# A 4096 x 4096 x 4096 matmul with bias and tanh: the first bias load, the matmuls on zeros, the place of one sum, and the order of all engines

## The chip, the cores and the metric

The kernel runs on one NeuronCore of a Trainium2 chip, in one launch. The metric is the device time of one execution in microseconds (us), as the median of several runs. The core has a matrix engine (TensorE, PE in the profile, with its weight loads as PEld), a vector engine (VectorE, DVE), a scalar engine (ScalarE, ACT), GpSimd (POOL) and SyncE (SP). Here GpSimd issues all loads of `a` and `b` from the inputs (converting them to fp16 on the way), and SyncE issues all other transfers: the bias, stores of results, and intermediate tiles to and from DRAM. Both feed the core's 16 DMA engines.

## The reference

```python
m, k, n = 4096, 4096, 4096
a = np.random.randn(m, k).astype(np.float32)
b = np.random.randn(k, n).astype(np.float32)
bias = np.random.randn(n).astype(np.float32)

def reference(a, b, bias):
    return np.tanh(np.matmul(a, b) + bias)
```

## The kernel before

**Arithmetic.** The kernel multiplies in fp16 with fp32 sums, by a scheme of the Strassen-Winograd kind: a 2 x 2 block product with seven products P1 to P7 in place of eight. The left operands are a11, a12, a22 and the sums s1 to s4 (s1 = a21 + a22, s2 = s1 - a11, s3 = a11 - a21, s4 = a12 - s2); the right ones are b11, b21, b22 and the sums t1 to t4. P1 = a11 b11, P2 = a12 b21, P3 = s4 b22, P4 = a22 t4, P5 = s1 t1, P6 = s2 t2, P7 = s3 t3. A product is either *plain* (for two row pairs, 2 x 16 matmuls of 128 x 128 by 512 columns, L832) or *fine*: the scheme is used once more inside it, with 7 x 8 matmuls of 256 columns (L847), and VectorE and ScalarE then make the inner sums (`fine_left`, `fine_right`).

**Tiling.** The columns of the output are cut into four chunks of 1024. The rows are cut into 16 pairs, and two pairs make a *duo*, eight in all.

- *Opening* (to about 121 us): the first eight row blocks of chunk 0 are computed by ordinary matmuls (L2049), while loads are short. It begins with `WARM` matmuls on a tile of zeros (L1968). Then come the first four tiles of each of four row blocks: they are loaded as `first` (L1975), turned on TensorE (L2088), copied out of PSUM by ScalarE and VectorE (L2094), and multiplied. Further rows are loaded as `land` and turned on VectorE (L506).
- *Chunk 0* (to about 404 us): the six remaining duos, in the order `ORDER[0]`. `STEEP[0]` says how many of a duo's products are fine: 1 means P1; 2 means P1 and P7; 3 means P1, P7 and P5. For each duo the rows of `a` are loaded (`nat`, L530), turned on VectorE and summed. s2 is made in the place of a11, and a copy of it goes to DRAM for the later chunks (`keep`, `move`, L594). s4 is made in `work`, when P3's turn comes, and is written over s2.
- *Chunks 1 and 2* (to about 1078 us) are done together, with 512-column matmuls inside fine products (L1572). They go product by product over all duos in `WIDE_ORDER`.
- *Chunk 3*: `pass_one` (P1, P2 and P6 of all duos) and `pass_two` (P7, P5, P4 and P3), in `ORDER[3]` and its reverse. Partial results wait in a tile `st` per duo; the last `HOLD` duos of the first pass keep it on the chip, the others send it to DRAM. In the second pass a duo has a `p7` and a `cs` tile besides. With `TOGETHER[3]` = n the last n duos of the second pass are run product by product, not duo by duo.

**What sets the order.** The code does not emit instructions directly. It adds operations to a `Plan`: engine, guessed duration, what is read and written, bytes. The plan gives each a due time, counted back from the end, and then plays the whole kernel through with its guesses: on each engine it takes the ready operation that is due first and for which there is room. Room is `PLACES` = 51 places of 4 KB per partition. From this come the order of the instructions on every engine and the place of each buffer. So a changed constant can move instructions everywhere. `WARM_TIME`, `RATES`, `SLACK` and the rest are guesses that enter only this play. `WIDE_EARLY`, `FARTHER` and the like say how far ahead of TensorE a load may be taken up. The chip knows only the resulting order on each engine and the waits that follow from what the operations read and write. An `after=` in `add` counts in the play alone, and makes no wait on the chip.

**Where the change sits.** `load_bias` (L919) is called for chunk 0 with `after=plan.last_pe`, when the first products of the opening have been added. `take_up` and `after_p1` are its first users. `KEEP_AT` says after which duo of chunk 0 the operands of the first two pairs go to DRAM: those pairs were turned in the opening (tiles named `o`).

Of the kernel before, what the change touches and what calls it, by code (L numbers as in the profile page):

```python
# [10 lines left out]
P = 128  # L11
QP = 32
NB = 512
NH = NB // 2
NCW = 2 * NB
# [1 line left out]
TB = 4  # L17
TP = T // 2
G = 2
WARM = 24  # L20
fp32 = mybir.dt.float32
fp16 = mybir.dt.float16
pair32 = mybir.dt.uint32
# [1 line left out]
SUB = mybir.AluOpType.subtract  # L25
# [5 lines left out]
KEPT = (('a11', 'a12'), ('s1', 'a22', 's4'), ('a11', 'a12', 's3', 's2', 's1', 'a22', 's4'), ())  # L31
NEAR = 10.0
REACH = 15.0
ORDER = ((2, 3, 4, 5, 6, 7), (7, 0, 4, 2, 6, 1, 3, 5), (2, 1, 4, 0, 3, 5, 6, 7), (7, 6, 5, 4, 0, 2, 1, 3))
LASTING = ((), (), (), ())
SHARED = True
SOFT = 1.5
BEHIND = 2
FARTHER = (50, 65, 40, 50)
THREE = (False, True, True, True)  # L40
AFTER = (6, 6, 6, 7)
HOLD = (1, 1, 1, 3)
KEEP_AT = (0, 1)
NAT_LEAD = 2.0
FIRST = (0, 1)
WHOLE = ()
# [2 lines left out]
HELD = ("s1", "s3", "s4")  # L49
PLAIN = (0, 0, 0, 0)  # L50
SMALL = 4
OVER = True
TWICE = True
RING = 8
SPEED, SLACK = 1.0, 0.8
# [8 lines left out]
    ((0.32, 0.40, 0.45), (0.47, 0.55, 0.54)),  # L64
)
FIRST_AT = 1.4
WARM_TIME = 7.6
RISE = ((), (4, 4, 4, 4, 4, 4, 4, 4), (4, 4, 4, 4, 4, 4, 4, 4), (4, 4, 4, 4, 4, 4, 4, 4))
SECONDS = (0, 8, 8, 8)
STEEP = ((0, 1, 2, 2, 2, 3), (), ())  # L70
BASIS = ("a11", "a12", "a22", "s2")
STORED = BASIS + ("s1", "s3", "s4")
LEFT = ('P6', 'P7', 'P5', 'P4', 'P3')
Q_ORDER = (0, 2, 1, 3)
WIDE = 1
WIDE_LASTING = ('s3', 's1')
TOGETHER = (0, 0, 0, 0)
WIDE_ORDER = (7, 6, 1, 5, 4, 3, 2, 0)
WIDE_PASSES = ((("P1", 0),), (("P2", 0),), (("P6", 0), ("P7", 1)), (("P4", 0),), (("P5", 0), ("P3", 1)))
TURN = 5  # L80
WIDE_EARLY = {'P1': (11.0, 80), 'P2': (11.0, 90), 'P6': (11.0, 100), 'P7': (8.0, 120), 'P4': (11.0, 70), 'P5': (11.0, 50), 'P3': (18.0, 100)}


class Buf:
# [74 lines left out]
class Plan:  # L159
# [14 lines left out]
    def add(self, eng, dur, emit, reads=(), writes=(), nbytes=0, hw=True, soft=None, early=0.0, lead=0.0, reach=1e9, after=None, long=False):  # L174
        early, far = early if isinstance(early, tuple) else (early, self.FAR)
        op = Op()
        op.n, op.eng, op.dur, op.emit = len(self.ops), eng, dur, emit
        op.nbytes, op.hw, op.soft, op.early, op.lead = nbytes, hw, soft, early, lead
        op.parts = 4 if dur > 1 and not hw else 1
        op.reach, op.far = reach, far  # L180
        if nbytes:
            kind = ("POOL", "LONG")[long] if not hw else "out" if soft is not None else "in"
            rate, wait = RATES[self.open][kind]
            op.flow, op.wait = nbytes / (rate * SPEED), wait + SLACK
            op.share = SHARES[self.open][long]
            op.kind = 0 if soft is None else 2 if writes else 1
        op.lag = op.wait + op.flow if nbytes else self.LATE
        preds, seen = set(), {}
        for group, writing in ((reads, False), (writes, True)):
            for access in group:  # L190
                buf, atoms = access if isinstance(access, tuple) else (access, access.atoms)
                if isinstance(buf, Bank):
                    if eng == "PE":
                        preds |= buf.rest
                        buf.rest = set()
                        buf.pe = op
                        buf.writer, buf.readers = {}, {}
                        continue
                    if buf.pe:
                        preds.add(buf.pe)  # L200
                    buf.rest.add(op)
                else:
                    seen[buf] = True
                for i in atoms:
                    if i in buf.writer:
                        preds.add(buf.writer[i])
                    if writing:
                        preds.update(buf.readers.get(i, ()))
                        buf.writer[i], buf.readers[i] = op, []
                    else:  # L210
                        buf.readers.setdefault(i, []).append(op)
        if after:
            preds.add(after)
        preds.discard(op)
        op.bufs = [b for b in seen if b.cls]
        for b in op.bufs:
            b.users += 1
        if eng == "PE":
            if self.last_pe:
                preds.add(self.last_pe)  # L220
            self.last_pe = op
        op.preds = preds
        op.succs = []
        for p in sorted(preds, key=lambda p: p.n):
            p.succs.append(op)
        self.ops.append(op)
        return op
# [181 lines left out]
def kernel(  # L409
# [7 lines left out]
    nc = tc.nc  # L417
# [43 lines left out]
    LO, HI = ds(0, NH), ds(NH, NH)  # L461
# [4 lines left out]
    def dve(n, emit, reads, writes, wide=False, **kw):  # L466
        add("DVE", 0.08 + n / (960 if wide else 1900), emit, reads, writes, **kw)
# [14 lines left out]
    ALL = slice(None)  # L482
# [137 lines left out]
    def asum(s, name, x, y, op, over=None, **kw):  # L620
        x, y = s[x], s[y]
        s[name] = s[over] if over else new(name, [P, T, P], atoms=2)
        tt(at(s[name]), at(x), at(y), op, T * P, (x, y), (s[name],), wide=False, **kw)
# [289 lines left out]
    def load_bias(c, after=None):  # L913
        k = {}
        k["b1"] = new("bias", [P, 2, NB], fp32, atoms=2)
        src = bias[ds(c * NCW, NCW)]
        add(
            "SP", 0.34,
            lambda: nc.sync.dma_start(  # L919
                out=k["b1"][ALL].rearrange("P a b -> P (a b)"),  # L920
                in_=bass.AP(tensor=src.tensor, offset=src.offset, ap=[[0, P], *src.ap]),
            ),
            (), (k["b1"],), nbytes=P * NCW * 4, after=after,
        )
        return k

# [19 lines left out]
    def work(duo, name, s, part=None, last=True):  # L946

        d, c, k, bop, pair = duo, duo.c, duo.k, duo.bop, duo.pairs[s]
        left, right, bank = {
            "P1": ("a11", "b11", D), "P2": ("a12", "b21", D), "P7": ("s3", "t3", I), "P6": ("s2", "t2", Z),  # L950
            "P5": ("s1", "t1", C), "P3": ("s4", "b22", C), "P4": ("a22", "t4", Z),
        }[name]
        bank = bank[s]
        a_ = d.a[s]
        if name == "P3" and "s4" not in a_:
            asum(a_, "s4", "a12", "s2", SUB, over=None if d.stays else "s2")
            if "s4" in d.put:
                put_by(d, "s4", s)
                if s:
                    sigma("s4", pair // 2, d.a, 12.0)  # L960
        t0, nt = (0, T) if part is None or name == "P3" else (part * TP, TP)
        start = name == "P1" or (name == "P7" and part != 1)
        product(bank, a_[left], [bop.get((right, i)) for i in range(4)], t0, nt, start)
        b1 = k["b1"]
        if name == "P1":
            after_p1(d, s, part)
        elif name == "P7":
            if part != 0:
                d.p7[s] = new("p7", [P, NB], fp32, "out")
                copy(at(d.p7[s]), at(bank), NB, (bank,), (d.p7[s],))  # L970
                after_p7(d, s, part)
        elif name == "P6":
            after_p6(d, s, part)
        elif name == "P5":
            if part == 0:
                return
            after_p5(d, s)
        elif name == "P2":
            if part == 0:
                e = d.aside[s] = [new("aside", [P, NB], fp32, "out" if i == 2 else "big") for i in range(0)]  # L980
                d.as11[s] = (d.box[s], 0)
                copy(at(d.box[s], ALL, 0), at(bank), NB, (bank,), ((d.box[s], (0,)),))
            else:
                finish(bank, 2 * pair, c * NCW)
        elif name == "P3":
            finish(bank, 2 * pair, c * NCW + NB)
        elif name == "P4":
            if part == 0:
                box, low = d.box[s], d.low
                tt(at(low, ALL, s), at(bank), at(box, ALL, 0), SUB, NB, (bank, (box, (0,))), ((low, (s,)),))  # L990
                tt(at(box, ALL, 1), at(C[s]), at(box, ALL, 0), SUB, NB, (C[s], (box, (0,))), ((box, (1,)),))
            else:
                finish(bank, 2 * pair + 1, c * NCW)
# [280 lines left out]
    def third(c, pq, pairs, fine):  # L1274

        duo = min(pairs) // 2
        after = c + 1 < NC and RISE[c + 1][ORDER[c + 1][::-1].index(duo)] < 4
        if {"P7", "P4"} <= set(fine) and {("a22", duo), ("s2", duo)} <= skewed and not after:
# [686 lines left out]
    def warm():  # L1965
        ps = psum.tile([P, NB], fp32, name="warm", tag="ps_0")
        for i in range(WARM):
            nc.tensor.matmul(ps[ALL], zeros[ALL, :P], zeros[ALL], start=i == 0, stop=i == WARM - 1)  # L1968

# [176 lines left out]
    for p in FIRST:  # L2146
# [3 lines left out]
        firsts[p] = s  # L2150
        if not KEEP_AT[p]:
            keep(p, s)
# [8 lines left out]
    k, before, held = k0, None, None  # L2161
    for c in range(NC):
# [14 lines left out]
        if c >= TWO:  # L2177
            plan.open = 2
            k = load_bias(c)
# [27 lines left out]
        for i, pairs in enumerate(duos):  # L2207
            d = Duo()
# [6 lines left out]
            over = OVER and 0 < i < len(duos) - 1  # L2215
# [68 lines left out]
```

## Time and profile before

| | |
|---|---|
| time before, median of 3 runs | 1433.62 us (1432.93 to 1434.62) |
| the profiled execution: its own time | 1433.78 us |
| the profiled execution: span, first to last instruction | 1432.1 us |
| TensorE matmuls | 1422.2 us busy, 99% of the span |
| VectorE | 1078.1 us, 75% |
| ScalarE | 392.8 us, 27% |
| GpSimd | 325.3 us, 23% |
| DMA | 399.19 MB, mean 279 GB/s |

The times in rows of the profile are microseconds from the start of the span. A timeline row gives the start, the length, the engine, the source line, the operation, `out<-in` by tile names without numbers, and how many instructions the row stands for. In brackets is how long the engine was idle before it, and what ended that. A wait on several things is put down to the one that came last. `SPq` rows are the issues of transfers by SyncE's queue. Lines of one helper (L473 is VectorE's two-operand operation, L476 ScalarE's copy) serve many purposes, so the tile names tell them apart. The ends of matmuls are modelled; their starts are not.

### The profile page before, as it was taken

What the parts mean: (1) busy time and instruction counts of PE and PEld (TensorE: products, weight loads), DVE (VectorE), ACT (ScalarE), POOL (GpSimd) and SP (SyncE); (2) the same over time, 40 slices, a digit from 0 to 9 for tenths busy, and PEclk for the clock granted to TensorE, in tenths of its full rate; (3) what the DMA queues carried; (4) which work ended last, traced back from release to release, by engine and by line L of the source; (5) the groups of instructions that cost most, each with busy time, mean ns of one, the idle gap of its engine ahead of it and who ended that gap; (6) DMA issues with size and microseconds to landing.
All of it is one profiled execution on the core that took longest, in us unless ns stands there. A gap on an engine that the chain in (4) does not pass through costs nothing.

```text
span 1432.1 us, 22563 instructions
## 1 busy us (share of the span) xinstructions
PE 1422.2 (99%) x8408; PEld 822.2 (57%) x8408; DVE 1078.1 (75%) x1594; ACT 392.8 (27%) x746; POOL 325.3 (23%) x613
## 2 busy tenths in 40 slices
PE   9999999999999999999999999999999999999998
PEld 4444555555644444444444444444447888888887
DVE  3359968767985376796568787988798689997876
ACT  3111212221333333311111133233233332244433
POOL 8764332334452341100111130000130300000000
PEclk9999999999999999999999999999999999999999
DMA  9999998899999899997899799899999987788883
GB/s 188 178 236 286 251 293 196 222 240 221 274 276 316 235 274 302 280 358 290 265 291 294 270 294 389 341 367 344 334 335 354 271 248 265 250 297 286 304 301 134
DMA packets 167486, 399.19 MB, mean 279 GB/s; under 512 B 25425, under 2 KB 44369, under 8 KB 167377
## 3 DMA queue, kind: packets, MB, share of 16 engines
q1 hardware_dynamic: 104400, 318.03, 61.2%
q0 software_dynamic: 62976, 79.73, 33.4%
q8 instruction: 66, 1.08, 0.3%
q14 instruction: 44, 0.35, 0.1%
HBM read 327.68 MB, written 149.68 MB: 333 GB/s over the span
## 4 chain that ended last, share of the span: by engine, by line
PE 76%; DMA 2%; DVE 1%; POOL 0%; issue 0%; ACT 0%; SPq 0%; DVEq 0%
PE ps L1572 45%; PE ps L847 25%; PE ps L832 6%; DMA nat<-in_a_dram 1%; DMA xa<-a 1%; DMA s<-a 1%; DVE a L473 0%; POOL nat L530 0%; DVE s L473 0%; DVE a L506 0%; DVE u L473 0%; ACT parts L1370 0%; DVE ys L473 0%; DVE parts L473 0%; DVE za L684 0%
## 5 line engine op out<-in xcount | busy, mean ns | idle before, releaser
L759 POOL DMA_DIRECT2D b<-in_b_dram x320 | 169.7, 535 | 607.7 <-DMA out_dram<-u 163.6
L476 ACT COPY ps<-ps 128x256 f32<-128x256 f32 (+1 forms) x216 | 100.8, 467 | 443.0 <-PE ps L1572 306.0
L530 POOL DMA_DIRECT2D nat<-in_a_dram x224 | 118.5, 533 | 208.8 <-DMA nat<-in_a_dram 51.6
L473 DVE TENSOR_TENSOR u<-ps,u 128x512 f32<-128x512 f32 x160 | 106.1, 686 | 26.2 <-PE ps L1572 25.1
L473 DVE TENSOR_TENSOR parts<-ps,parts 128x512 f32<-128x512 f32 (+1 forms) x129 | 72.6, 563 | 67.2 <-PE ps L1572 40.0
L832 PEld LDWEIGHTS <-a 128*128 128x128 f16 x704 | 68.8, 98 | 81.9 <-issue 2.4
L473 DVE TENSOR_TENSOR ps<-ps,parts 128x256 f32<-128x256 f32 (+1 forms) x151 | 82.7, 552 | 39.4 <-PE ps L1572 22.0
L2049 PE MATMUL ps<-b,o 128*128 128x512 f16 x512 | 111.3, 379 | 0.1
L476 ACT COPY parts<-ps 128x256 f32<-128x256 f32 (+1 forms) x151 | 69.0, 461 | 135.9 <-DVE ps L473 45.6
L1572 PE MATMUL ps<-b,zs 128*128 128x512 f16 x448 | 105.8, 379 | 0.0
L1572 PEld LDWEIGHTS <-ya 128*128 128x128 f16 x624 | 61.1, 98 | 73.6
L506 DVE STREAM_TRANSPOSE a<-nat 128x512 uint32<-128x512 uint32 x112 | 73.2, 690 | 20.8 <-DMA nat<-in_a_dram 17.4
L832 PE MATMUL ps<-b,a 128*128 128x512 f16 x384 | 84.7, 379 | 2.1 <-DVE parts L473 2.1
L1572 PEld LDWEIGHTS <-zs 128*128 128x128 f16 x512 | 50.1, 98 | 60.2
L1572 PEld LDWEIGHTS <-xa 128*128 128x128 f16 x512 | 50.1, 98 | 60.2
L2049 PEld LDWEIGHTS <-o 128*128 128x128 f16 x512 | 49.8, 98 | 60.3 <-ACT o L2094 0.5
L494 ACT ACTIVATE parts<-ps 128x512 f32<-128x512 f32 x52 | 31.0, 597 | 162.4 <-PE ps L832 98.1
L1572 PE MATMUL ps<-b,za 128*128 128x512 f16 x320 | 75.6, 379 | 0.0
L473 DVE TENSOR_TENSOR b<-b,b 128x2048 f16<-128x2048 f16 (+2 forms) x76 | 68.0, 910 | 10.1 <-DMA b<-in_b_dram 9.5
L832 PE MATMUL ps<-t,a 128*128 128x512 f16 x320 | 72.3, 379 | 0.0
L1572 PEld LDWEIGHTS <-za 128*128 128x128 f16 x384 | 37.6, 98 | 45.3
L847 PEld LDWEIGHTS <-ya 128*128 128x128 f16 x592 | 57.9, 98 | 7.1
(163 smaller groups left out, 2560.1 us busy)
## 6 DMA issues: line engine op xcount, KB each, us to landing
b<-in_b_dram POOLq DMA_DIRECT2D x320, 128.0 KB, 8.0
ya<-a SPq DMA_DIRECT2D x70, 512.0 KB, 7.2
xa<-a SPq DMA_DIRECT2D x70, 512.0 KB, 7.2
u<-U SPq DMA_DIRECT2D x62, 512.0 KB, 6.6
nat<-in_a_dram POOLq DMA_DIRECT2D x224, 128.0 KB, 8.0
U<-u SPq DMA_DIRECT2D x48, 512.0 KB, 6.9
ys<-s SPq DMA_DIRECT2D x46, 512.0 KB, 5.0
xs<-s SPq DMA_DIRECT2D x46, 512.0 KB, 5.6
```

The costliest lines, as they stand in the source:

```text
L473: dve(n, lambda: nc.vector.tensor_tensor(out=o(), in0=x(), in1=y(), op=op), reads, writes, wide, **kw)
L476: act(n, lambda: nc.scalar.copy(o(), x()), reads, writes, **kw)
L494: act(NB, lambda: nc.scalar.activation(o[ALL], src[ALL], TANH), (src,), (o,), soft=2.0)
L506: nc.vector.transpose(dst[ALL].rearrange("P t m -> P (t m)").bitcast(pair32).rearrange("P (U m) -> P U m", m=P)[:, ds(t0 // 2, nu), ds(row ...
L530: nc.gpsimd.dma_start(out=tl[(ds(q * QP, QP), *key)], in_=src)
L759: nc.gpsimd.dma_start(out=dst.rearrange("p t j n -> p t (j n)") if j is None else dst, in_=src)
L832: nc.tensor.matmul(bank[ALL], left_tile(left, k + t + shift), rb.tile(t), start=start and k == t0 and t == 0, stop=k + t == t0 + nt - 1, s ...
L847: nc.tensor.matmul(bank[ALL, HALF[half]], left_tile(buf, at_ * TP + i * TB + t), rb.tile(t), start=False, stop=i == 1 and t == TB - 1, ski ...
L1572: nc.tensor.matmul(bank[ALL, cols], left_tile(buf, at_ * TP + i * TB + t), rb.tile(t, half), start=start and not (i or t), stop=i == 1 and ...
L2049: nc.tensor.matmul(bank[ALL], left_tile(left, t), rb.tile(tb), start=start, stop=stop, skip_group_check=True,)
```

## The change

- The first chunk's bias: a memset of 256 columns of the bias tile is added on VectorE, planned after the last TensorE operation added so far, and the load writes the same tile, so that the load waits for the memset. The load itself no longer carries `after`.
- `WARM` goes from 24 to 18 matmuls on zeros, and its guessed time from 7.6 to 6.3 us.
- s4 in chunk 0 is written over a12, not over s2.
- `STEEP[0]`: the third duo has one fine product in place of two.
- `KEEP_AT`: the operands of pair 1 go to DRAM when they are made, not after the first duo.
- `ORDER[3]`, `TOGETHER[3]`, `FARTHER[3]`, three entries of `WIDE_EARLY`, and no `SLACK` on transfers in the opening: they act through the plan alone.

```diff
-WARM = 24
+WARM = 18
...
-ORDER = ((2, 3, 4, 5, 6, 7), (7, 0, 4, 2, 6, 1, 3, 5), (2, 1, 4, 0, 3, 5, 6, 7), (7, 6, 5, 4, 0, 2, 1, 3))
+ORDER = ((2, 3, 4, 5, 6, 7), (7, 0, 4, 2, 6, 1, 3, 5), (2, 1, 4, 0, 3, 5, 6, 7), (5, 2, 1, 4, 0, 6, 7, 3))
...
-FARTHER = (50, 65, 40, 50)
+FARTHER = (50, 65, 40, 40)
...
-KEEP_AT = (0, 1)
+KEEP_AT = (0, 0)
...
+S4_OVER = 'a12'
...
-WARM_TIME = 7.6
+WARM_TIME = 6.3
...
-STEEP = ((0, 1, 2, 2, 2, 3), (), ())
+STEEP = ((0, 1, 1, 2, 2, 3), (), ())
...
-TOGETHER = (0, 0, 0, 0)
+TOGETHER = (0, 0, 0, 3)
...
-WIDE_EARLY = {'P1': (11.0, 80), 'P2': (11.0, 90), ..., 'P3': (18.0, 100)}
+WIDE_EARLY = {'P1': (14.0, 100), 'P2': (11.0, 50), ..., 'P3': (14.0, 90)}
...
-            op.flow, op.wait = nbytes / (rate * SPEED), wait + SLACK
+            op.flow, op.wait = nbytes / (rate * SPEED), wait + SLACK * (self.open > 0)
...
         k["b1"] = new("bias", [P, 2, NB], fp32, atoms=2)
         src = bias[ds(c * NCW, NCW)]
+        if after:
+            dve(NH, lambda: nc.vector.memset(k["b1"][ALL, 0, HI], 0.0), (), (k["b1"],), after=after)
         add(
             "SP", 0.34,
...
-            (), (k["b1"],), nbytes=P * NCW * 4, after=after,
+            (), (k["b1"],), nbytes=P * NCW * 4,
...
         if name == "P3" and "s4" not in a_:
-            asum(a_, "s4", "a12", "s2", SUB, over=None if d.stays else "s2")
+            asum(a_, "s4", "a12", "s2", SUB, over=None if d.stays else S4_OVER)
```

More of the change, by code (lines that the diff above doesn't have):

```diff
@@ L80 @@
 TURN = 5
-WIDE_EARLY = {'P1': (11.0, 80), 'P2': (11.0, 90), 'P6': (11.0, 100), 'P7': (8.0, 120), 'P4': (11.0, 70), 'P5': (11.0, 50), 'P3': (18.0, 100)}
+WIDE_EARLY = {'P1': (14.0, 100), 'P2': (11.0, 50), 'P6': (11.0, 100), 'P7': (8.0, 120), 'P4': (11.0, 70), 'P5': (11.0, 50), 'P3': (14.0, 90)}
 class Buf:
```

## The prediction

> **What bounds the kernel now.** I read the page first, then the list of what TensorE (PE) waited for, and then the timeline around each of those waits.
>
> ```profile
> span 1432.1 us, 22563 instructions
> PE 1422.2 (99%) x8408; PEld 822.2 (57%) x8408; DVE 1078.1 (75%) x1594; ACT 392.8 (27%) x746; POOL 325.3 (23%) x613
> ...
> PE ps L832 <- DVE parts L473: 2.1, 1, 2.1
> PE ps L847 <- DVE a L473: 1.7, 1, 1.7
> PE warm L1968 <- DVE zeros L1962: 1.4, 1, 1.4
> PE ps L847 <- ACT ps L476: 0.4, 1, 0.4
> ```
>
> TensorE is busy for 1422.2 of 1432.1 us, so the kernel is bound by its matmuls and only 9.9 us are idle. The list names 5.6 of them: 1.4 before the first matmul on zeros, two stalls in the first chunk (2.1 and 1.7) and one of 0.4 near the start of the last chunk. Most of the rest is the tail behind the last matmul, which this change does not shorten. So whatever the new order does, it can win only three things: fewer or cheaper matmuls, the head, and 4.2 us of stalls. It can lose anything, since an order set anew can bring new stalls in any stage.
>
> The profiled execution took 1433.78 us, 1.68 more than its span. I make the sum against 1433.78 and take off 0.16 at the end, the distance to the median of 1433.62. About 0.2% (2.87 us) is what a measurement of this kernel can tell from no change, so faster means below 1430.75 and slower above 1436.49.
>
> **The matmuls: a step of STEEP.** The third duo of chunk 0 goes from two fine products to one, so its P7 becomes plain. The timeline shows both kinds back to back:
>
> ```profile
> 317.54 10.52 PE L832 MATMUL ps<-b,a 128*128 128x512 f16 x48
> 327.90 1.04 PE L847 MATMUL ps<-b,a 128*128 128x256 f16 x8
> 328.78 1.04 PE L847 MATMUL ps<-f1t,ys 128*128 128x256 f16 x8
> ```
>
> By starts, 48 plain matmuls take 327.90 - 317.54 = 10.36 us, 0.2158 each; 8 fine ones 0.88 us, about 0.1093 each over longer runs. The fine P7 is 7 x 8 = 56 matmuls, 6.12 us; the plain one 2 x 16 = 32, 6.91 us. That is **+0.79 us**, all on TensorE and so on the path. No other constant changes the number of products. In exchange VectorE (DVE) loses the duo's fine left sides; the splitting of t3 for the first fine P7 is not saved, it moves to the next duo.
>
> **The two stalls in chunk 0: s4 in a12's place.** The timelines around them:
>
> ```profile
> 239.04 1.96 SPq L594 DMA_DIRECT2D s<-a  x1
> 250.45 1.23 DVE L473 TENSOR_TENSOR a<-a,a 128x2048 f16<-128x2048 f16 x1 [4.55 <-DMA s<-a]
> 251.59 0.68 DVE L473 TENSOR_TENSOR parts<-ps,parts 128x512 f32<-128x512 f32 x1
> 252.33 3.61 PE L832 MATMUL ps<-b,a 128*128 128x512 f16 x16 [2.11 <-DVE parts L473]
> 254.78 3.67 POOL L530 DMA_DIRECT2D nat<-in_a_dram  x7 [9.62 <-DVE parts L473]
> ...
> 272.53 1.30 DVE L506 STREAM_TRANSPOSE a<-nat 128x512 uint32<-128x512 uint32 x2 [2.73 <-DMA nat<-in_a_dram]
> 279.75 1.23 DVE L473 TENSOR_TENSOR a<-a,a 128x2048 f16<-128x2048 f16 x1
> 281.04 1.05 PE L847 MATMUL ps<-b,a 128*128 128x256 f16 x8 [1.71 <-DVE a L473]
> ```
>
> The operation at 250.45 is s4 = a12 - s2, written over s2. In this duo s2 lies in an a11 buffer, and its copy to DRAM (s from a) is still being read, so VectorE stands for 4.55 us. Queued behind it is the sum that ends P5 (251.59) and frees the bank for P3, and TensorE loses 2.11 us. The same block holds a buffer that GpSimd (POOL) waits for: 9.62 us in which no rows of `a` are requested. Those rows are the ones that VectorE then waits for at 272.53, and from there its work runs on to the s3 of the next duo (279.75), for which TensorE stands 1.71 us. One wait, two stalls.
>
> Written over a12, s4 waits for a12's readers instead: P2, which TensorE runs before P7, and a store that the code asks for ahead of that of s2. Neither is late here. What becomes due next at 250 is P3 itself, with nothing missing. The plain P7 acts on the same spot and gives the stores 0.79 us more. I take **-2.11**. For the second stall the rows of `a` can be asked for some 4 us sooner (the 4.55 us of the block), more than the 1.71 us missing, so I take **-1.71**. Bounds: each lies between nothing and all of it. Against the second stands that t3's split, 16 differences of the kind below, now falls into the next duo, in front of its P7:
>
> ```profile
> 229.93 1.43 DVE L473 TENSOR_TENSOR b<-b,b 128x512 f16<-128x512 f16 x4
> ```
>
> That is 16 x 0.36 = 5.7 us of VectorE; in the old place they hid beside P1, P2 and P7 itself without a stall. If they land before the s3, the 1.71 us stays.
>
> **The head: 18 matmuls on zeros, and the bias moved.**
>
> ```profile
> 0.81 0.38 SPq L919 DMA_DIRECT2D bias<-in_bias_dram  x1
> 1.34 0.87 POOL L1975 DMA_DIRECT2D first<-in_a_dram  x1 [0.82 <-POOLq L2268]
> 1.40 7.63 PE L1968 MATMUL warm<-zeros 128*128 128x512 f16 x24 [1.40 <-DVE zeros L1962]
> 5.65 0.15 PEld L1968 LDWEIGHTS <-zeros 128*128 128x128 f16 x1 [0.28 <-issue]
> 6.07 2.47 PEld L1968 LDWEIGHTS <-zeros 128*128 128x128 f16 x12 [0.27 <-issue]
> 6.12 0.77 POOL L1975 DMA_DIRECT2D first<-in_a_dram  x1
> 10.86 0.27 PEld L2088 LDWEIGHTS <-first 128*128 128x128 f16 x4 [0.28 <-DMA first<-in_a_dram]
> 11.82 0.12 PEld L2049 LDWEIGHTS <-o 128*128 128x128 f16 x2 [0.53 <-ACT o L2094]
> ...
> DMA to landing us min/median/max: 4.3/4.8/5.0
> ...
> q0 software_dynamic: 541, 0.19, 57.9%
> q1 hardware_dynamic: 133, 0.48, 53.1%
> ```
>
> The first matmuls on zeros start 0.43 us apart, up to 6.07, the later ones at the full rate. The six taken away are of the fast kind: 6 x 0.2158 = 1.29 us, so the zeros end at 7.74 in place of 9.03. But that is not what sets the start of the products. The fourth piece of `first` is issued at 6.12, its transposes wait for it until 10.86, and the last row's matmuls wait for their ScalarE (ACT) copy until 11.82. With the zeros gone sooner TensorE waits at the same places. Moving the bias helps little: between 2 and 5 us (the two queue rows) its 0.48 MB share the engines with only 0.19 MB of the loads, which mostly come after it. The bound is the unloaded landing: 6.12 + 4.3 = 10.42, at most 0.44 us sooner. So the head gives between 0 and -0.44 if GpSimd's issues stay where they are, and at most the -1.29 of the zeros if the new order moves them up. I take **-0.2**, nearer the landing row than the matmul row.
>
> The bias in its new place: a memset, bounded by the row at 1.07 below, goes ahead of it on VectorE. It waits for its turn there, not for TensorE, so it is only as late as the VectorE work planned around it.
>
> ```profile
> 1.07 0.27 DVE L1962 MEMSET zeros<- 128x256 uint32 x1
> 33.89 2.72 DVE L506 STREAM_TRANSPOSE o<-land 128x256 uint32<-128x256 uint32 x8
> 45.99 1.43 DVE L506 STREAM_TRANSPOSE o<-land 128x256 uint32<-128x256 uint32 x4 [9.39 <-DMA land<-in_a_dram]
> 49.85 3.11 DVE L473 TENSOR_TENSOR ps<-spill,bias 128x512 f32<-128x512 f32 x5 [2.44 <-ACT spill L476]
> 88.28 2.06 SPq L487 DMA_DIRECT2D out_dram<-parts  x3
> ...
> out_dram<-parts SPq DMA_DIRECT2D x20, 256.0 KB, 14.2
> ```
>
> Issued about 31 to 37 us, behind the first products, it is needed at 49.85. SyncE (SP) has nothing queued behind it until 88.28. Even with the 14.2 us that stores take in a crowded stretch (80 to 162 us) it lands by 51.2, 1.3 us late at worst; VectorE's 9.39 us of idleness covers the memset. I cost it at nothing, with up to 1.3 us in the range.
>
> **The rest of the new order.**
>
> ```profile
> 160.33 4.81 SPq L594 DMA_DIRECT2D a<-o  x6
> ...
> 100.00:110.00 10.00, 10.00 (x48) 4.58 (x47) 10.00 (x17) 1.79 (x3) 4.74 (x9) 1.00 1.09 308
> ```
>
> KEEP_AT moves pair 1's eight stores (these six, 0.8 us each to issue, and two more, some 2.1 MB) from 160 us to about 90 to 110, ahead of output stores on SP and beside the loads of `a` on GpSimd's queue. VectorE (third engine of the second row) is busy for all 10 us there and waits for no transfer; that backlog hides them. Without it the loads would come 2.1 MB / 308 GB/s = 6.8 us later.
>
> WIDE_EARLY, FARTHER and the missing slack shift loads within the cover that leaves TensorE no stall from 281 to 1127 us. The 0.4 us at 1127 lies where ORDER[3] changes the sequence: I take **-0.2**, between nothing and all. TOGETHER runs the last three duos product by product: the same matmuls, at nothing if their buffers fit (third rival).
>
> Sum: +0.79 - 2.11 - 1.71 - 0.2 - 0.2 = -3.43, so 1430.35 for an execution like the profiled one and **1430.2 us** for the median. With the head and the last stall at their ends (-1.29 and -0.45, or nothing) this case alone runs from 1428.9 to 1430.6.
>
> **Rivals.** *First, a stall comes back.* The split of t3, or loads placed by a plan that no longer adds slack in the opening, make TensorE stand once or twice for about what is removed: 1430.2 + 1.71 = 1431.9, with the 2.11 too 1434.0. For it: VectorE is at 75% over the whole span, and each stall above came from a chain that the plan had not seen. Against: one cause made both stalls.
>
> *Second, the clock falls in the head.* Between 7.74 and 11.82 us TensorE would have 16 transposes and a few matmuls. If that counts as idle, the next matmuls start 0.43 us apart again for as long as at first, 6.07 - 1.40 = 4.67 us: 11 in place of 21.6, so 10.6 x 0.2158 = 2.3 us, 1432.5. The Trainium skill, TensorE: Matmul & The Clock Gate, Part 1 (The HAM clock gate), says that the clock halves after about one idle window of 3.4 us; by that rule this would be it, if the transposes do not count. Against: after the 2.11 us gap at 252.33 sixteen matmuls took 3.61 us, the full rate.
>
> *Third, slower: the last three duos do not fit.* Run together they hold three sets of `st`, `p7` and `cs` in place of one, six more of 51 places. In the last 173 us the operand loads on SP already wait for TensorE to give places back:
>
> ```profile
> SPq L594 <- PE ps L847: 42.8, 29, 5.2
> ...
> xs<-s SPq DMA_DIRECT2D x17, 512.0 KB, 5.5
> ...
> 1123.43 1.23 DVE L684 TENSOR_TENSOR za<-xa,ya 128x2048 f16<-128x2048 f16 x1 [2.19 <-DMA xa<-a]
> ```
>
> If a load can start only when the product before it begins, its landing (5.5) and its sum (1.23) make 6.73 us against 6.12 of product: 0.61 us lost in each of 15 products, 9.2 in all, 1439.4. It decides as soon as fewer than one product's operands are held ahead. Against: TensorE has no stall there now, and no right sides are loaded any more.
>
> **How the numbers follow.** Forecast 0.50, first rival 0.30, second 0.05, third 0.15. The forecast is faster throughout, the first two rivals lie within 0.2%, the third is slower: 0.50, 0.35, 0.15. The range goes from 1428.6, just under the forecast's low end, to 1437.0, past the first rival with the late bias on top; it leaves out the third rival and little else.
>
> **What would show it.** Right: no TensorE wait on VectorE between 240 and 290 us; the s4 sum without a DMA wait; GpSimd without its 9.6 us gap; TensorE's busy time near 1421.7; the zeros ending near 7.7 but the last transposes still waiting for `first` at 10.4 to 10.9. Wrong: a head shorter by over a microsecond, a bias that lands after 50 us, loads at 0.43 us spacing after the zeros, or stalls in chunk 0, at the change of passes, or in the last 130 us.

## The result and the profile after

| | before | after |
|---|---|---|
| median of 7 runs each | 1433.2 us (1432.16 to 1434.62) | 1437.56 us (1436.52 to 1440.94) |
| profiled execution | 1433.78 us | 1438.08 us |
| its span | 1432.1 us | 1436.4 us |

The ratio is 1.0033 [1.0021, 1.0045], so the changed kernel is slower by 0.33%, about 4.7 us (the two medians differ by 4.36). The forecast was 1430.2 us, faster than before; the measurement lies 0.6 us above the top of the range. The page of the changed kernel, first and third line, and then its list of TensorE's waits (total, times, longest):

```profile
span 1436.4 us, 22490 instructions
...
PE 1424.0 (99%) x8378; PEld 819.6 (57%) x8378; DVE 1071.6 (75%) x1588; ACT 389.8 (27%) x740; POOL 326.5 (23%) x613
```

```profile
PE ps L833 <- ACT ps L477: 2.8, 1, 2.8
PE ps L848 <- DVE a L474: 1.7, 1, 1.7
PE warm L1971 <- DVE zeros L1965: 1.4, 1, 1.4
PE ps L2052 <- DVE ps L2077: 0.8, 1, 0.8
PE tp L2091 <- DMA first<-in_a_dram: 0.6, 1, 0.6
PE ps L2052 <- DVE ps L474: 0.3, 1, 0.3
```

Thirty matmuls have gone from the list, as forecast for the plain P7 (24) and the zeros (6), and yet TensorE is busy for longer: 1424.0 us, where the prediction looked for 1421.7. Of the old stalls the 2.1 and the 0.4 are gone. A 1.7 by the same kind of sum is still there, but at another place, and a 2.8 is new. The timeline of the changed kernel shows where:

```profile
10.84 20.64 PE L2052 MATMUL ps<-b,o 128*128 128x512 f16 x92
32.30 20.88 PE L2052 MATMUL ps<-b,o 128*128 128x512 f16 x96 [0.82 <-DVE ps L2077]
53.50 69.23 PE L2052 MATMUL ps<-b,o 128*128 128x512 f16 x320 [0.32 <-DVE ps L474]
122.56 7.07 PE L833 MATMUL ps<-b,a 128*128 128x512 f16 x32
132.47 8.75 PE L833 MATMUL ps<-b,a 128*128 128x512 f16 x32 [2.84 <-ACT ps L477]
141.06 3.62 PE L833 MATMUL ps<-b,s 128*128 128x512 f16 x16
...
263.80 1.04 PE L848 MATMUL ps<-b,a 128*128 128x256 f16 x8
...
332.39 1.05 PE L848 MATMUL ps<-b,a 128*128 128x256 f16 x8 [1.75 <-DVE a L474]
```

A way to read two such timelines is to follow how far a matmul of one kernel lags behind the same matmul of the other:

| place | before, us | after, us | lag, us |
|---|---|---|---|
| products of the opening run on | 11.18 | 10.84 | -0.34 |
| opening done, chunk 0 begins | 121.12 | 122.56 | +1.44 |
| end of P1 of the first duo | 134.94 | 141.06 | +6.12 |
| past the old stall of 2.11 | 259.24 | 263.80 | +4.56 |
| past the old stall of 1.71 | 307.98 | 310.56 | +2.58 |
| a later duo's P7 | 327.90 | 332.39 | +4.49 |
| end of chunk 0 | 404.19 | 409.04 | +4.85 |
| end of the span | 1432.1 | 1436.4 | +4.3 |

So the two stalls were won as forecast (the lag goes from 6.12 down to 2.58, even with the plain P7 in between). The loss is made before 141 us, and 1.9 us of the gain are given back at a later P7.

What delayed TensorE at 132.47? The timeline of the changed kernel for SP's queue, VectorE, ScalarE and GpSimd:

```profile
88.87 2.92 SPq L595 DMA_DIRECT2D a<-o  x3
92.58 0.32 SPq L595 DMA_DIRECT2D s<-s  x1
92.94 1.11 SPq L488 DMA_DIRECT2D out_dram<-parts  x2
...
97.92 14.94 SPq L488 DMA_DIRECT2D out_dram<-parts  x8
...
123.80 0.69 DVE L474 TENSOR_TENSOR parts<-a 128x1024 f16<-128x1024 f16 x1 [4.60 <-DMA out_dram<-parts]
...
131.15 0.67 DVE L474 TENSOR_TENSOR ps<-ps,bias 128x512 f32<-128x512 f32 x1
131.85 0.57 ACT L477 COPY ps<-ps 128x512 f32<-128x512 f32 x1 [3.39 <-DVE ps L474]
...
129.98 4.22 POOL L531 DMA_DIRECT2D nat<-in_a_dram  x8 [8.65 <-DMA out_dram<-parts]
```

Before, SP issued three output stores at 88.28 and only then the first operand copy (`a` from `o`, 90.38). Now pair 0's four operand stores of 512 KB (three of `a`, one of `s`) go first, because the plan has no slack, and pair 1's, which `KEEP_AT` moved, stand among the output stores behind them: at 94.76, 95.66 and 114.54, two at 118.07 and more. The chain of waits (start, length, what) runs through them:

```profile
90.88 6.96 DMA a<-o
...
97.92 16.56 DMA out_dram<-parts
...
114.54 12.37 DMA a<-o
...
131.85 0.58 ACT ps L477
...
132.47 2.64 PE ps L833 x7
```

The copy issued at 90.88 lands 6.96 us later, at 97.84, and just then the run of eight output stores starts; the first of these lands after 16.56 us, at 114.48, and just then pair 1's copy of 114.54 goes out. In both cases the later transfer is the eighth after the earlier one on SP. The trace has this for every issue from 97.92 to 132.71: each comes less than 0.1 us after the landing of the transfer eight places ahead of it. So at most eight transfers are under way on SP's queue here (the plan assumes the same, `RING = 8`), and each one that is put in early holds back all that come behind it.

Each store that lands frees a 4 KB place for a tile of results (`parts`). VectorE needs such a place for a sum and stands 4.60 us for a store, the one issued at 108.92. All that is behind that sum in VectorE's order comes later, down to the sum with the bias (131.15) that TensorE needs; before, that one came at 124.78, and VectorE waited for no transfer between 100 and 130 us. The chain goes on from pair 1's copy of 114.54 to sums of `b` at 126.94. I read no wait there: VectorE came to those sums straight from the sum before, and that copy landed only at 128.8.

The 2.84 us are not the whole price. The next 32 matmuls take 141.06 - 132.47 = 8.59 us by starts, against 6.91 at the full rate. The weight loads and the windows of the changed kernel (busy time of PE, PEld, DVE, ACT and POOL, then the granted clock, the share of DMA and GB/s) show why:

```profile
133.63 0.15 PEld L833 LDWEIGHTS <-a 128*128 128x128 f16 x1 [0.28 <-issue]
134.05 0.15 PEld L833 LDWEIGHTS <-a 128*128 128x128 f16 x1 [0.28 <-issue]
```

```profile
128.00:132.00 4.00, 1.63 (x8) 0.65 (x7) 4.00 (x8) 0.61 (x2) 2.02 (x4) 1.00 1.05 405
132.00:136.00 4.00, 3.53 (x10) 1.35 (x10) 3.96 (x5) 0.91 (x2) 2.20 (x5) 0.63 1.07 321
136.00:140.00 4.00, 4.00 (x19) 1.73 (x18) 4.00 (x7) 0.68 (x2) 1.33 (x3) 0.95 1.10 277
```

They are 0.43 us apart, and 10 matmuls start in the middle window, where 19 do in the next one. The granted clock, 0.63 in the middle window, costs 1.68 us more. Slow matmuls count as busy, which is why TensorE's busy time rose.

### The profile page after: what moved, and what is told of

It is laid out like the page before. It is cut to its first block, busy times and chain, and to the rows that moved or that the text cites. A ratio compares the mean times of both kernels' runs of the same rounds, so it can differ in the third digit from the quotient of the medians.

```text
span 1436.4 us, 22490 instructions
## 1 busy us (share of the span) xinstructions
PE 1424.0 (99%) x8378; PEld 819.6 (57%) x8378; DVE 1071.6 (75%) x1588; ACT 389.8 (27%) x740; POOL 326.5 (23%) x613
## 4 chain that ended last, share of the span: by engine, by line
PE 89%; DMA 7%; DVE 2%; POOL 2%; issue 1%; ACT 0%; DVEq 0%; POOLq 0%; SPq 0%; ACTq 0%
PE ps L1575 47%; PE ps L848 27%; PE ps L833 15%; DMA b<-in_b_dram 2%; DMA out_dram<-parts 2%; DMA land<-in_a_dram 1%; DMA a<-o 1%; POOL b L760 1%; POOL land L531 1%; DVE a L507 0%; DVE o L507 0%; DVE ps L2077 0%; POOL first L1978 0%; DVE ps L474 0%; DVE b L474 0%
## 5 line engine op out<-in xcount | busy, mean ns | idle before, releaser
L477 ACT COPY ps<-ps 128x512 f32<-128x512 f32 (+1 forms) x215 | 100.4, 467 | 451.4 <-PE ps L1575 309.6
L474 DVE TENSOR_TENSOR parts<-ps,parts 128x256 f32<-128x256 f32 (+1 forms) x128 | 72.0, 563 | 83.5 <-PE ps L1575 38.9
L833 PEld LDWEIGHTS <-a 128*128 128x128 f16 x800 | 78.7, 98 | 95.4 <-issue 5.8
L833 PE MATMUL ps<-b,a 128*128 128x512 f16 x480 | 107.9, 383 | 2.9 <-ACT ps L477 2.8
```

What stands on the lines that cost most here:

```text
L474: dve(n, lambda: nc.vector.tensor_tensor(out=o(), in0=x(), in1=y(), op=op), reads, writes, wide, **kw)
L477: act(n, lambda: nc.scalar.copy(o(), x()), reads, writes, **kw)
L833: nc.tensor.matmul(bank[ALL], left_tile(left, k + t + shift), rb.tile(t), start=start and k == t0 and t == 0, stop=k + t == t0 + nt - 1, s ...
```

## The experiments

Each ratio is to the kernel before on the same chip, with its 95% interval.

**The stores late again.** In the changed kernel:

```diff
-KEEP_AT = (0, 0)
+KEEP_AT = (0, 1)
```

> The changed kernel with KEEP_AT = (0, 1) again: pair 1's eight stores go out after the first duo. Theory K (the early stores push the output stores back, these free their places late, VectorE stands at 119 to 124 us, TensorE stands 2.8 us at 130 and then runs 32 matmuls at a lower clock): the stall and the clock loss go, some 4.5 us less than the changed kernel, about 1433.0. Theory S (it is the missing slack in the opening that hands out places too early): no change, 1437.5. The plan is made anew, so other stalls can move by a microsecond or two.

1435.22 us, ratio 1.0005 [0.9996, 1.0015], clear of the changed kernel's interval. There is no stall near 130 us, and the opening ends at 121.47; new stalls of 0.94 and 1.24 stand at 153.66 and 327.73. This edit moves the order of all engines, though, so the next kernel holds it.

**The same order, without the early stores.** In the changed kernel the eight early store instructions are left out, and the same bytes are sent from a tile of zeros at about 165 us instead. So pair 1's rows of chunks 1 to 3 are computed from zeros.

```diff
+if p == 1:
+    for op in plan.ops[n:]:
+        op.emit = lambda: None
...
+if op.start > 165 and not sent:
+    ...
+    nc.sync.dma_start(out=box[ALL, first_, ds(4 * h, 4)], in_=zeros[ALL]...)
```

> The changed kernel with the order of everything else held: pair 1's eight stores are left out at their early place and as many bytes are stored from a tile of zeros at about 165 us, so the rows of pair 1 in chunks 1 to 3 are computed from zeros. Theory K: VectorE no longer waits 4.6 us for an output store near 120 us, the 2.8 us stall and the clock loss go, about 1433.0. Theory S: the place is still handed out too early, 1437.5 or at most a microsecond less.

1434.51 us, 1.0007 [0.9996, 1.0018]. The timeline of this kernel at the place of the loss:

```profile
120.71 0.69 DVE L474 TENSOR_TENSOR parts<-a 128x1024 f16<-128x1024 f16 x1 [0.84 <-DMA out_dram<-parts]
...
122.48 14.22 PE L833 MATMUL ps<-b,a 128*128 128x512 f16 x64
```

Every instruction that is left stands in the same order, and VectorE's wait for the output store shrinks from 4.60 to 0.84 us. TensorE has neither gap nor slow stretch. So the stores themselves make the loss near 130 us, not the rest of the order. The stall near 32 us stays (0.89) and that of 1.7 at 330 too, with one of 1.4 at 206 us; these are not theirs. The opening still ends at 122.48.

**The slack back in the opening.** In the changed kernel, stores still early:

```diff
-            op.flow, op.wait = nbytes / (rate * SPEED), wait + SLACK * (self.open > 0)
+            op.flow, op.wait = nbytes / (rate * SPEED), wait + SLACK
```

> The changed kernel with the plan's 0.8 us of slack on transfers put back in the opening. Theory K: the eight stores are still early, the stall near 130 us stays within a microsecond, 1436 to 1438. Theory S: the stall and the clock loss go and also the two short ones (0.8 at 31 us, 0.3 at 53 us), 1432 to 1433.

1432.4 us, 0.9991 [0.9982, 1.0000]. The plan now puts output stores first on SP, and P1 of the first duo has no stall. The timeline of this kernel:

```profile
89.71 2.06 SPq L488 DMA_DIRECT2D out_dram<-parts  x3
...
122.56 13.98 PE L833 MATMUL ps<-b,a 128*128 128x512 f16 x64
```

Pair 1's 2.1 MB still move early, so that alone does not make this loss. But their first store is issued at 106.35, behind the ninth output store (99.78); in the changed kernel two of them (94.76, 95.66) and all of pair 0's stand ahead of the ninth. Nor is it enough that pair 0's stores go first, as they do with the stores late, too (three copies of `a` at 87.83). The stall near 130 us needs both. The slack sets the order of all engines anew, so what else it does is not separated. The head of this kernel shows something else, weighed with the 24 zeros below.

**s4 in a12's place alone,** in the kernel before:

```diff
-            asum(a_, "s4", "a12", "s2", SUB, over=None if d.stays else "s2")
+            asum(a_, "s4", "a12", "s2", SUB, over=None if d.stays else "a12")
```

> The kernel before with one edit: s4 in chunk 0 is written over a12. The prediction's theory: both stalls (2.1 at 250 us, 1.7 at 279 us) come from s4's wait for the store of s2, so both go: 1433.2 - 3.8 = 1429.4. Rival (the plain P7 of the third duo was needed too, or the freed place is now s2's and comes late): one of them stays, 1431 to 1433.

1433.71 us, 0.9996 [0.9986, 1.0006]. Both stalls at 250 and 279 us are gone, and two others appear. This kernel's timeline:

```profile
234.95 0.38 PE L847 MATMUL ps<-f2t,ys 128*128 128x256 f16 x2 [0.56 <-DVE f2t L473]
...
251.66 3.62 PE L832 MATMUL ps<-b,a 128*128 128x512 f16 x16
...
365.60 1.30 DVE L506 STREAM_TRANSPOSE a<-nat 128x512 uint32<-128x512 uint32 x2 [2.50 <-DMA nat<-in_a_dram]
373.94 1.05 PE L847 MATMUL ps<-b,a 128*128 128x256 f16 x8 [1.68 <-DVE a L473]
```

P3 (251.66) starts without a gap, but at 365.60 VectorE waits for rows of `a` again, and the next P7 behind it stands 1.68 us. Of 3.8 us removed, 2.2 come back in the profile, and the median is 0.4 us below that of the kernel before, which its interval does not tell from nothing.

**The early stores alone,** in the kernel before:

```diff
-KEEP_AT = (0, 1)
+KEEP_AT = (0, 0)
```

> The kernel before with one edit: KEEP_AT = (0, 0), pair 1's eight stores sent when its operands are made. Theory K alone: the stores push the output stores back by themselves, a stall of 2.8 us near 130 us and 1.7 us of clock behind it: 1433.6 + 4.5 = 1438. Theory K and S together (only a plan without slack puts three of these stores ahead of the first output stores on SyncE's queue): no such stall, within a microsecond of the kernel before.

1440.98 us, 1.0043 [1.0028, 1.0058]: alone they cost about as much as the whole change, but neither theory had the place. There is no gap at 130 us; it lies at 161.73. The timeline of this kernel, then its windows:

```profile
160.45 1.22 DVE L473 TENSOR_TENSOR s<-a,s 128x2048 f16<-128x2048 f16 x1
161.73 6.58 PE L832 MATMUL ps<-b,s 128*128 128x512 f16 x16 [5.29 <-DVE s L473]
```

```profile
158.00:162.00 4.00, 0.27 (x1) 0.13 (x2) 3.97 (x6) 0.00 (x0) 0.89 (x3) 0.87 1.08 329
162.00:166.00 4.00, 4.00 (x11) 1.40 (x10) 3.96 (x10) 0.63 (x1) 2.08 (x4) 0.50 1.08 318
```

TensorE waits 5.29 us for an s4 that is written over s2. VectorE is busy all the time and waits for no transfer: s4 simply stands behind other work in its order. Its 16 matmuls then run at half rate (6.58 in place of 3.62). My reading is that the plan guessed the store of s2, now behind more stores on SP, as landing late, and so gave s4 a late turn. Played through by itself, the plan of this kernel says so: its guess for that landing is 160.7 us, where the kernel before has 152.1, and its guess for s4 is 161.3 in place of 152.2. On the chip the store (issued at 142.86, 13.9 us to landing) was in by 156.8, before s4 had its turn. The next kernel, and further down the one with s4 over s2 again, test what follows from it.

**Early stores and s4 in a12's place,** in the kernel before (the two diffs above together):

> The kernel before with two edits: pair 1's eight stores early and s4 in a12's place. Alone the stores cost 6.7 us: s4 of the first duo came 5.3 us late, since the store of s2 lies behind them. If that is the cause, s4 over a12 takes the stall and the clock loss away: 1432 to 1434. Rival (the stores delay the rows of `a` as well, or the plan's order shifts the wait elsewhere): 1436 or more.

1433.86 us, 1.0006 [0.9996, 1.0015]. s4 comes at 152.81, and in place of the gap of 5.29 there is one of 0.43. Others of 0.6, 0.6 and 1.8 stand at 240, 279 and 375 us. The edit that alone was worth nothing that shows is worth some 5 to 7 us here (from 1.0043 to 1.0006, or 1440.98 to 1433.86).

**The bias early, the order held.** In the changed kernel the memset is left out, so that the load has nothing to wait for and goes at 0.8 us:

```diff
-dve(NH, lambda: nc.vector.memset(k["b1"][ALL, 0, HI], 0.0), (), (k["b1"],), after=after)
+dve(NH, lambda: None, (), (k["b1"],), after=after)
```

> The changed kernel with the order of everything held and the memset of the bias left out, so the bias goes out at once, at 0.8 us, as before the change. If the late bias costs nothing (its memset runs at 37 us, after the 0.8 us stall at 31 us), the time stays within 0.7 us of the changed kernel, 1437 to 1438. Rival: 0.5 MB beside the loads of the opening costs the 1.4 us that the products of the opening end later: about 1436. In the head the pieces of `first` should land up to 0.4 us later, if the bias was in their way.

1437.71 us, 1.0022 [1.0013, 1.0032]: not to be told from the changed kernel. The stalls at 32, 53, 131 and 330 us are all there, so none of them is the bias. The products of the opening start at 11.20, 0.36 later than in the changed kernel, about what was expected of the bias; but with the late bias and 18 zeros they also started at 11.08 and 11.28 in two kernels, so one profile does not show it.

**24 zeros, the order held,** in the changed kernel:

```diff
-WARM = 18
+WARM = 24
```

> The changed kernel with 24 matmuls on zeros and the order of everything held. If the six were not on the path (the pieces of `first` set the pace), the start of the steady products stays at 10.8 us plus at most 0.3 and the time within 0.7 us, 1437 to 1438. Rival (the second of the prediction: with 18 the clock falls in the head in a part of the executions, which then lose 1.5 to 2 us): the median falls by about a microsecond, to 1436.5, and weight loads 0.43 us apart behind the zeros are never seen.

1436.79 us, 1.0018 [1.0008, 1.0029], overlapping the changed kernel's. The steady products start at 11.28, a little later than expected, and the median lies between what the two theories gave, so it does not tell them apart. The gap near 130 is there in this execution too, but the clock did not fall after it (this kernel's timeline):

```profile
131.93 7.27 PE L833 MATMUL ps<-b,a 128*128 128x512 f16 x32 [2.50 <-ACT ps L477]
```

**The slack back and 24 zeros.** In the changed kernel, the slack's diff above and

```diff
-WARM = 18
+WARM = 24
-WARM_TIME = 6.3
+WARM_TIME = 7.6
```

> The changed kernel with the slack in the opening and the 24 matmuls on zeros (guessed at 7.6 us) put back. From the run with slack alone: there TensorE stood 2.6 us in the head and the clock fell, the opening ended 1.4 us later than before the change. If the zeros cover that gap, 1432.4 - 1.4 = 1431.0, faster than the kernel before by about 0.2%. Rival (the later rows of `a` set the pace anyway, what is won in the head is given back at the P7 of a later duo): 1432.4.

1430.95 us (1429.97 to 1432.32), 0.9976 [0.9966, 0.9986]: the first kernel that is clearly faster than the one before. Its list of TensorE's waits is nearly empty:

```profile
PE warm L1971 <- DVE zeros L1965: 1.4, 1, 1.4
PE ps L848 <- DVE ps L474: 1.1, 2, 0.6
PE ps L2052 <- DVE o L2097: 0.3, 1, 0.3
```

It beats the slack alone by 1.45 us, though the intervals just overlap, so the worth of the six zeros is not settled. The heads, one execution each, fit it. With 18 zeros and the slack (first of the two timelines) TensorE stood for a piece of `first`, and then loaded weights 0.43 us apart for a while:

```profile
6.58 0.39 PE L2091 MATMUL tp<-ident,first 128*128 128x128 f16 x4
9.61 0.41 PE L2091 MATMUL tp<-ident,first 128*128 128x128 f16 x4 [2.64 <-DMA first<-in_a_dram]
...
13.28 0.15 PEld L2052 LDWEIGHTS <-o 128*128 128x128 f16 x1 [0.27 <-issue]
```

With 24 zeros no such stretch follows, and the opening ends at 121.51 in place of 122.56:

```profile
1.40 8.02 PE L1971 MATMUL warm<-zeros 128*128 128x512 f16 x24 [1.40 <-DVE zeros L1965]
```

**Three more steps from that kernel.** The bias at the start again:

```diff
-        if after:
-            dve(NH, lambda: nc.vector.memset(k["b1"][ALL, 0, HI], 0.0), (), (k["b1"],), after=after)
...
-            (), (k["b1"],), nbytes=P * NCW * 4,
+            (), (k["b1"],), nbytes=P * NCW * 4, after=after,
```

> The faster version (the changed kernel with the slack and 24 zeros put back, 1430.95) with the bias loaded at the start again, as before the change. If the bias's place is worth nothing: 1431 within 0.7 us. If the bias in the head holds the first pieces up by its 0.4 us: 1431.4; if beside the loads at 37 us it costs more than in the head: 1430.5 or less.

1431.37 us, 0.9981 [0.9970, 0.9991]: the place of the bias makes no difference that shows. s4 over s2 again:

```diff
-S4_OVER = 'a12'
+S4_OVER = 's2'
```

> The faster version with s4 over s2 again. The early stores stay, so by the run with the stores alone s4 of the first duo waits for its s2's store: a stall of some 5 us near 160 us and 1.5 us of clock, 1437 or more. Rival (with the plain P7 of the third duo and the new order s4 has time): 1431 to 1433.

1438.95 us, 1.0041 [1.0026, 1.0056]. The gap of the early stores alone is back, at the same place and with the same half rate behind it. This kernel's timeline:

```profile
161.35 1.22 DVE L474 TENSOR_TENSOR s<-a,s 128x2048 f16<-128x2048 f16 x1
162.63 6.09 PE L833 MATMUL ps<-b,s 128*128 128x512 f16 x16 [6.08 <-DVE s L474]
```

With early stores s4 over a12 is thus worth about 8 us. And the step of `STEEP` undone:

```diff
-STEEP = ((0, 1, 1, 2, 2, 3), (), ())
+STEEP = ((0, 1, 2, 2, 2, 3), (), ())
```

> The faster version with two fine products in the third duo again. By the count of matmuls 0.79 us less of TensorE, 1430.2, if nothing waits. Rival (the rows of `a` and VectorE set the pace of chunk 0, the fine P7 brings VectorE's work and a stall back): no gain or 1 to 2 us more, 1431 to 1433.

1430.7 us, 0.9979 [0.9970, 0.9989]. The two fine products save matmuls and bring a stall of 0.67 us at 239.86; the time is not to be told from that with the plain P7.

## Why the prediction was wrong, step by step

**The failed step: KEEP_AT at nothing.** The prediction said of pair 1's eight stores that VectorE's "backlog hides them". That VectorE was busy and waited for no transfer between 100 and 110 us was true, and is true after. The step that failed is what the backlog was taken to cover. I wrote that the stores go "ahead of output stores on SP", but priced only what they delay beside them (the loads of `a`), and not what is queued behind them: output stores, whose landing frees the places into which VectorE writes 25 us later. The row that named it was quoted: an output store took 14.2 us to land there. Measured in the profiled execution: a VectorE wait of 4.60, a TensorE gap of 2.84 and 1.68 of slow clock, 4.5 us in all.

The traces let the dose be followed. The store that VectorE waits for is the ninth output store on SP, and VectorE is ready for its place at 119 to 120 us:

| kernel | ninth output store issued | landed | VectorE waits for it | TensorE's gap near 130 us |
|---|---|---|---|---|
| before | 98.75 | 114.2 | no | none |
| slack back | 99.78 | 116.4 | no | none |
| stores late | 103.68 | 119.2 | no | none |
| same order without the early stores | 105.39 | 120.6 | 0.84 | none |
| changed, bias early | 107.66 | 122.2 | 3.43 | 1.39 |
| changed, 24 zeros | 108.36 | 123.1 | 4.09 | 2.50 |
| changed | 108.92 | 123.7 | 4.60 | 2.84 |

Its way from issue to landing is 14.5 to 16.6 us in all of them, so it lands late because it is issued late. Two of pair 1's stores stand ahead of it in the changed order, and leaving them out brings its issue forward by 3.5 us. The missing slack is the other half: it puts all four of pair 0's operand stores in front. The prediction put it at nothing, too, by cover "from 281 to 1127 us", though the slack is taken off in the opening alone, which ends at 121. Either one undone removes the loss (the stores 1.0005 or 1.0007, the slack 0.9991, against 1.0033). The last three rows have the same order, so the gap differs between executions (1.39 to 2.84), and only the longest of the three was followed by the slow clock; by the ratios with the order held the early stores are worth about 0.26%, 3.7 us.

**The opening.** +1.78 us between 10.84 and 122.56 were not in the sum: 0.82, 0.32 and a pause of 0.57 between weight loads at 14.02. The early stores are not its cause: without them, in the same order, the opening ends at 122.48 (with the stall near 32, without that near 53), and with the early bias at 122.55. With the stores late and the order made anew, or with slack and 24 zeros, it ends within 0.4 us of the kernel before (121.47, 121.51, against 121.12). What the stall near 32 us waits for can be read on VectorE, first in the kernel before, then in the changed one:

```profile
29.14 4.84 DVE L2074 COPY ps<-spill 128x512 f32<-128x512 f32 x8
```

```profile
30.87 0.78 DVE L507 STREAM_TRANSPOSE o<-land 128x256 uint32<-128x256 uint32 x2 [1.29 <-DMA land<-in_a_dram]
31.57 4.81 DVE L2077 COPY ps<-spill 128x512 f32<-128x512 f32 x8
```

TensorE needs the copies. The order made without slack puts two more transposes ahead of them, and these wait for a load of `a` to land. With the stores late the same two stand there and TensorE has no gap, since they run 0.76 us earlier and TensorE comes 0.4 us later; so the order alone does not decide it.

**The stalls at 250 and 279 us: right.** -3.54 us of lag with the plain P7's +0.79 in it, against -3.03 forecast (where the 0.5 us beyond it come from was not traced). Between 240 and 290 us TensorE has no stall in the changed kernel, VectorE waits 0.5 us for a transfer where it waited 7.3, and GpSimd waits for TensorE alone. But "what becomes due next" was looked for in one place only. The next P7s come from the same chain, rows of `a` through VectorE: at 320.59 its transposes wait 4.42 us for an output store, and the P7 at 332.39 stands 1.75. The edit alone gave nothing that shows.

**STEEP: right** in size: the plain P7 runs from 249.98 to 256.89, the 6.91 us that were worked out; its worth in the best kernel was not resolved. **The head: right in what sets it,** since the last transposes still waited for `first` (0.59 us, to 10.58). The size, -0.34 against -0.2, is luck as far as one execution each can say: with the old head the products started at 11.18, 11.56, 11.76 and 11.80 in four kernels. The zeros ended at 8.08, not near 7.7, because the slow start lasted longer in that execution. **The late bias: right:** its load is issued at 37.42 and lands 6.7 us later, before its first use at 52.78, and bringing it forward changed nothing that shows. **The stall at 1127 us: gone,** -0.45.

**The rivals.** The first, a stall that comes back through "a plan that no longer adds slack in the opening", is what happened. Its price was off: 1.7 to 3.8 us were given to it, taken from the stalls removed. The measured loss over the forecast is 7.4. I let the new stalls be no longer than the old ones and gave none of them a slow clock. The second, the clock in the head, did not show in the changed kernel's profile, but did in that with slack and 18 zeros. Its argument against, full rate after a gap of 2.11 us, held for 2.11 us and was too short for the gaps that came. The third did not come: the last duos run without a stall, and from 404 us to the end the lag shrinks from 4.85 to 4.3.

**The whole.** With the slack and the six zeros put back, the rest of the change reaches 1430.95 us, 0.24% below the kernel before. That is close to the forecast's 1430.2, which is 0.24% below 1433.62, with the stalls of chunk 0 gone and the early stores in place. The nearness is in part luck: the sum's term for the head rests on the 18 zeros, which this kernel does not have, its opening ends 0.39 us later than before, and it has two stalls, 1.1 us together, that the sum did not have.

## What to carry to other kernels

When transfers are moved forward on a queue, price what stands behind them there, above all stores whose landing frees room: the one who pays may stand 30 us later on another engine. Where the queue is full, each transfer put ahead of the one that matters delays it by a step, about 1.8 us here. A stall removed in a chain that stays the slowest can be met again at the chain's next deadline, as it was here. An edit's worth can be nothing that shows alone and about 8 us beside another edit, so test it in both surroundings. Where TensorE would stand for more than about 2.5 us, add the slow matmuls after the gap to its price as a possibility.

## What the runs showed of the hardware

The granted clock falls after gaps shorter than I had allowed for, and not after each of about the same length. Matmuls ran at the full rate after 1.39, 2.11 and, in one execution, 2.50 us. After 2.64 (with a few transposes ahead of it), 2.84, 5.29 and 6.08 us they ran at about half rate, 0.43 us apart in place of 0.22. The Trainium skill, TensorE: Matmul & The Clock Gate, Part 1 (The HAM clock gate), puts the fall after about one idle window of 3.4 us. The gaps of 5.29 and 6.08 agree; those of 2.64 and 2.84 are shorter, and there the measurement decides.

After the two shorter gaps the fall came when work had already begun again. In the changed kernel the granted clock is 1.00 from 132.47 to 133.00, with three matmuls, 0.50 from 133.10 to 136.40, and 1.00 after that. With slack and 18 zeros TensorE works again from 9.61, and the clock is 0.50 from 10.90 to 14.20. After the gaps of 5.29 and 6.08, where it fell before work began again, it is 0.50 for twice as long (161.0 to 167.7, and to 167.6). So the four falls seen here came in two lengths: about 3.4 us at half rate, or 6.8.

The slow start varies between executions of the same instructions. In five profiles 18 zeros took 5.34 to 6.94 us, and in nine 24 took 6.94 to 8.26, depending on when the loads 0.43 us apart ended (3.94 in one, 7.34 in another). So spare zeros can cover a head that varies, which one profile does not show.
